# Block inversion through full matrices in DRAM on GpSimd's DMA queue, embeddings' projection by halves, all splits on VectorE

## The chip, the cores and the metric

One core of a Trainium2 chip runs one inference step of a hybrid decoder layer: a prompt of 1024 tokens and 8 sample sequences of 8 tokens. The metric is device time in microseconds, the median over runs; lower is better.

## The reference, cut to what matters

```python
proj = x @ w_in                                   # 1024 -> 3848
o_a, ... = _rwkv7_mix(proj[..., :A_SHIFT_W], ...) # 8 heads of 64: a recurrence over tokens
o_b, ... = _gated_delta_mix(proj[..., A_SHIFT_W:], ...)  # 4 heads of 128, chunks of 64
mix = concat([o_a, o_b]) @ w_o
x = _layer_norm(DN_ALPHA * x + mix, ln1_g, ln1_b)
ffn = (silu(conv(x @ w_gate_half) + b) * (x @ w_up_half)) @ w_down
x = _layer_norm(DN_ALPHA * x + ffn, ln2_g, ln2_b)
e = _rms_norm(p @ w_ple, ple_g)                   # the embeddings' projection
x = x + sigmoid(x @ w_ple_gate) * e
# inside _chunk_gated_delta, per chunk and head:
sol = triangular_solve(eye + Lmat, rhs, lower=True, unit_diagonal=True)
```

The kernel computes the recurrence of mixer A chunk by chunk as well, so both mixers need inverses of unit triangular matrices: per unit of work 24 systems of 64x64.

## The kernel before

**Precision.** A float32 product is made of three passes of float32r: an operand is split into hi and lo (`split`, L257: ACT copies hi, then a subtraction gives lo on VectorE or, without an engine named, on GpSimd). Weights come through `wchunk` (L385), split on VectorE.

**Stages.** The prompt is cut into two token blocks tb of 512. `proj` (L448) projects a block in one gate group and 14 groups of 256 columns (`proj_pair`, 48 matmuls of 128x512 per group) and stores the results to DRAM. The mixers work in units (tb, half, g): 256 tokens, half the heads; eight of them for the prompt, then two for the samples. A unit goes through `prep` (L1042: loads, convolutions, gates, `a_gram` with its Gram products L690, `b_gram`, `invert`), `merge` (L991), `scan` (L1064) and `mix_out` (L1082), which stores into od[tb]. In program order (`run`, L1647 to L1665) the scan of unit i runs with the merge of unit i+1, then comes the output of unit i, then the preparation of unit i+2. The tile framework lays out each engine's order of instructions when the kernel is built, by priorities; buffers of one tag go round in program order. PSUM has 4 banks with the tag acc, 2 aux and 2 scan. Preparation, merge and output all use the aux banks.

**Filler.** Work inside `with s.fill()` has the lowest priority and is to occupy TensorE between the mixers' steps: the projections, the embeddings' projection `ple` (L1364), after unit 3 the output projection `dense_first` of block 0 (L1657; its chunk k needs rows k of od[0], which units 2g and 4+2g store for both halves), then the last projection groups (L1658), `norm_first` and `ffn_first`, in which `ffn_tile` (L1439) copies two columns on GpSimd (L1442, L1444) for each of 22 tiles.

**Inversion.** `invert` (L942) takes a unit's 24 systems. It stores them to a DRAM tile dT (L955), loads their 16x16 diagonal blocks, 4 per system, as 96 rows into iN (L958), inverts all 96 blocks at once on VectorE (L959 to L966), makes a transposed copy (L972), stores both (L967, L973) and loads them back as diagonal blocks of Dd and Dt, 8 DMAs each (L987). The rest of Dd and Dt was set to zero once (L317). All these DMAs go out on the queue `s.uq = nc.scalar` (L311): ScalarE's. `merge` combines the blocks into the full inverse in four rounds of products; `touch` (L204) opens a round with a matmul that waits for the named DMAs. For a sample unit (`small`) the systems are 8x8 blocks, and the inverted blocks go straight into DX (L982, L985).

The embeddings' projection makes, for each token block and column half, one pass of `dense` (L1250) over 2 chunks, with 4 token tiles in 4 acc banks; the banks are emptied by ACT (L1388) at the pass's end.

Of the kernel before, what the change touches and what calls it, by code (L numbers as in the profile page):

```python
# [9 lines left out]
F32 = mybir.dt.float32  # L10
F32R = mybir.dt.float32r
AF = mybir.ActivationFunctionType
ALU = mybir.AluOpType
# [3 lines left out]
D = 1024  # L17
# [128 lines left out]
class Kern:  # L146
# [107 lines left out]
        else:  # L254
            s.act(out, out, AF.Exp, scale=-0.5, bias=s.cst[:p, post:post + 1])

    def split(s, hi, lo, raw, eng=None):  # L257

        s.act(hi, raw)
        s.tt(lo, raw, hi.bitcast(F32), ALU.subtract, eng or s.nc.gpsimd)  # L260

    @contextmanager
    def fill(s):
# [8 lines left out]
    def setup(s):  # L272
        nc, I = s.nc, s.I
        s.cst = s.tl([128, NCST], "cst", pool=s.cp)
        s.par = s.tl([128, NPAR], "par", pool=s.cp)
        s.w2 = s.tl([128, 512], "w2", pool=s.cp)
        s.g2 = s.tl([128, 512], "g2", pool=s.cp)
        nc.scalar.preload_act_table_set("exp_and_others")
        p0 = s.tc.cur_priority
        s.tc.cur_priority = p0 + 200  # L280
        nc.sync.dma_start(s.par, I["par"])
        nc.sync.dma_start(s.cst, I["cst"])
        nc.sync.dma_start(s.w2, I["w2"])
        nc.sync.dma_start(s.g2, I["g2"])
        s.ident = s.cst[:, C_ID:C_ID + 128]
        s.bones = s.cst[:, C_BO:C_BO + 128]
        s.ones = s.cst[:, C_ON:C_ON + 128]
        s.fold = s.cst[:, C_FO:C_FO + 64]
        s.omu = s.tl([128, 14], "omu", pool=s.cp)
        s.ts(s.omu, s.par[:, P_MU:P_MU + 14], -1.0, 1.0, ALU.mult, ALU.add)  # L290
        s.nkk = s.tl([128, 4], "nkk", pool=s.cp)
        s.ts(s.nkk, s.par[:, P_KK:P_KK + 4], -1.0)
        s.oka = s.tl([128, 4], "oka", pool=s.cp)
        s.ts(s.oka, s.par[:, P_KA:P_KA + 4], -0.5, 1.0, ALU.mult, ALU.add)
        s.hpar = s.tl([128, P_KA + 4 - P_W0 + 1], "hpar", pool=s.cp)
        s.ts(s.hpar[:, :P_KA + 4 - P_W0], s.par[:, P_W0:P_KA + 4], 0.5)
        s.ts(s.hpar[:, P_KA + 4 - P_W0:], s.par[:, P_NG:P_NG + 1], 0.5)
        s.eal = s.tl([4, 1], "eal", pool=s.cp)
        s.act(s.eal, s.par[0:4, P_AL:P_AL + 1], AF.Exp)
        s.ts(s.eal, s.eal, -1.0)  # L300
        s.tc.cur_priority = p0
        s.zeros = s.tl([128, 128], "zeros", dt=F32R, pool=s.cp)
        s.act(s.zeros, s.cst[:, C_BM:C_BM + 1].broadcast_to([128, 128]), AF.Copy, scale=0.0)
        s.tails = [s.tl([128, 26, 3], "tail%d" % i, pool=s.cp) for i in range(3)]
        nc.gpsimd.memset(s.tails[-1], 0.0)
        s.od = [s.tl([128, KT, n], "od%d" % i, pool=s.dp) for i, n in enumerate((TB, TB, 64))]
        s.uad = s.tl([128, 14, 8, 8], "uad", pool=s.dp)
        s.ubd = s.tl([128, 12, 8, 8], "ubd", pool=s.dp)
        s.zd = s.tl([128, 4, 64], "zd", pool=s.dp)
        s.SA, s.SB = [], []  # L310
        s.uq = nc.scalar  # L311
        s.iN = s.tl([96, 16, 16], "iN")
        s.iY = s.tl([96, 16, 16], "iY")
        s.it = s.tl([96, 56], "it")
        s.Dd, s.Dt = s.tl([128, 12, 64], "Dd"), s.tl([128, 12, 64], "Dt")
        s.DX = [s.tl([128, 12, LB], "DX%d" % i) for i in range(2)]
        for t in (s.Dd, s.Dt, *s.DX):  # L317
            nc.gpsimd.memset(t, 0.0)
        for g in range(2):
            for S in (s.SA, s.SB):  # L320
                S.append(s.tl([128, 2, 128], "S%d%d" % (g, S is s.SB)))
                nc.gpsimd.memset(S[g], 0.0)
# [33 lines left out]
    def load_x(s, src, more=None):  # L356

        x = s.xtiles()
        if not more and not s.late:
            for k in range(0, KT, 2):  # L360
                raw = s.tl([128, D], "X", 3, dt=F32R, pool=s.c0).bitcast(F32).rearrange("p (k t) -> p k t", k=2)
                s.nc.sync.dma_start(raw, src[:, k:k + 2, :])
                s.split(x[k // 2][:, 0], x[k // 2][:, 1], raw, s.nc.vector if k < 4 else None)
            return x
        for k in range(KT):
            raw = s.hraw() if s.late else s.st()
            with s.tc.high_priority() if more and k < 1 else ExitStack():
                s.nc.sync.dma_start(raw, src[:, k, :])
                s.split(*s.xk(x, k), raw, s.nc.vector if more else None)
                if more and k % 2 == 0:  # L370
                    more(k)
        return x

    def load_xs(s):
        x = s.tl([128, D], "X", 3, dt=F32R, pool=s.c0).rearrange("p (k i t) -> p k i t", k=KT, i=2)
        raw = s.tmp(128, KT, 64)

        def load(k):
            ks = slice(k, k + 2)
            s.nc.sync.dma_start(raw[:, ks], s.I["xT"][:, ks, T:T + 64])  # L380
            s.split(x[:, ks, 0, :], x[:, ks, 1, :], raw[:, ks], s.nc.vector)

        return x, load

    def wchunk(s, src, to=None):  # L385

        w = src.shape[-1]
        raw = s.wraw()
        hi, lo = to or (s.tl([128, 512], t, 3, dt=F32R, pool=s.mp) for t in ("whi", "wlo"))
        with s.tc.high_priority():  # L390
            s.nc.sync.dma_start(raw[:, :w], src)
            s.split(hi[:, :w], lo[:, :w], raw[:, :w], s.nc.vector)
        return hi, lo

    def proj_group(s, x, xs, wsrc, cuts, sample):
# [538 lines left out]
    def systems(s, sa, sb):  # L934

        for h in range(2):
            r = 64 * h
            yield h, 0, sa["MG"].rearrange("p c a s e t -> p (c a) s e t")[r:r + 64, :, 0, 1 - h, :]
            if r < sb["L"]:
                yield h, 2 * sa["nch"], sb["MB"][r:r + 64, :, :, 0, r:r + 64].rearrange("p q h t -> p (q h) t")  # L940

    def invert(s, sa, sb, small):  # L942

        nc = s.nc
        nch = sa["nch"]
        nb = 2 * sb["nq"]
        nh = 2 * nch + nb
        ns = nh + (2 * nch if small else nh)
        dT = s.tl([64, 24, 64], "inv_t", 2, pool=s.dp)
        d1, d2 = (s.tl([96, 16, 16], t, 2, pool=s.dp) for t in ("inv_x", "inv_y"))  # L950
        N, Y, tmp = s.iN, s.iY, s.it
        DX = s.DX[0]
        s.DX = s.DX[::-1]
        for h, y, t in s.systems(sa, sb):
            s.uq.dma_start(dT[:, h * nh + y:h * nh + y + t.shape[1], :], t)  # L955
        n = 4 * ns
        for k in range(4):
            s.uq.dma_start(N[k * ns:(k + 1) * ns], dT[16 * k:16 * k + 16, :ns, 16 * k:16 * k + 16].rearrange("r y t -> y r t"))  # L958
        nc.vector.tensor_copy(Y[:n], N[:n])  # L959
        for j in range(1, 15):  # L960
            m = 15 - j
# [2 lines left out]
            s.mul(t, N[:n, j:j + 1, j + 1:].broadcast_to([n, j, m]), y[:, :, j:j + 1].broadcast_to([n, j, m]))  # L964
            s.add(y[:, :, j + 1:], y[:, :, j + 1:], t)
        nc.vector.memset(Y[:n].rearrange("p a b -> p (a b)")[:, 0::17], 1.0)  # L966
        s.uq.dma_start(d1[:n], Y[:n])  # L967
        if small:
            nc.gpsimd.memset(DX, 0.0)
            todo = ((DX, d1, 64),)  # L970
        else:
            nc.vector.tensor_copy(N[:n], Y[:n].rearrange("p c i -> p i c"))  # L972
            s.uq.dma_start(d2[:n], N[:n])  # L973
            todo = ((s.Dt, d2, 0), (s.Dd, d1, 0))
        for D, d, w in todo:
            for h in range(2):
                for k in range(4):
                    rows = slice(64 * h + 16 * k, 64 * h + 16 * k + 16)
                    cols = slice(w * h + 16 * k, w * h + 16 * k + 16)
                    y = k * ns + h * nh  # L980
                    if small:
                        s.uq.dma_start(D[rows, :2 * nch, cols], d[y:y + 2 * nch].rearrange("y r t -> r y t"))  # L982
                        if h == 0:
                            y += 2 * nch
                            s.uq.dma_start(D[rows, 8:8 + nb, cols], d[y:y + nb].rearrange("y r t -> r y t"))  # L985
                    else:
                        i = s.uq.dma_start(D[rows, :, cols], d[y:y + nh].rearrange("y r t -> r y t"))  # L987
                        sa.setdefault("dma", []).append(i.ins)
        sa["DX"] = sb["DX"] = DX

    def merge(s, sa, sb):  # L991
# [8 lines left out]
        for k in range(4):  # L1000
            bs = [s.bank() for _ in range(2)]
            with s.inrow():
                s.touch(bs[0], s.nc.cur_bb.bb.instructions[-1], *(sa["dma"][8 * k:8 * k + 8] if k < 2 else ()))
                for i in range(12):
                    for h, r in enumerate(halves):
                        s.mm(bs[i // 8][r, i % 8 * 64:i % 8 * 64 + 64], DX[r, i, r] if k else T[h, i],
                             (Dt, Dd, Y, Y)[k][r, i, :])
# [313 lines left out]
    def transposed(s, xs, i, c0, x, tag, dst=None):  # L1321
# [5 lines left out]
        for k in range(0, KT, q):  # L1327
# [16 lines left out]
                hi, lo = (x[k // 2][:, e, :, cs] for e in range(2))  # L1344
                u = u.rearrange("p (k t) -> p k t", k=q)
            s.act(hi, u)
            s.tt(lo, u, hi.bitcast(F32), ALU.subtract, s.nc.gpsimd if (k // q) % 2 else None)

    def transposed_s(s, xs, i, tag):
        x = s.tl([128, KT, 2, 64], "xsm", dt=F32R)  # L1350
# [13 lines left out]
    def ple(s):  # L1364
        nc, I = s.nc, s.I
        for tb in range(3):
# [12 lines left out]
            for h in range(2):  # L1379
# [6 lines left out]
                def evac(t, b):  # L1386
# [1 line left out]
                    s.act(v, b)  # L1388
                    out(4 * tb + t, 128, v)

                s.dense(2, (lambda i: x[i]) if x else None, lambda i: I["w_ple"][h][:, i, :], evac,
                        None if x else (lambda i: xs[:, i]), lambda v: out(8, 64, v))

        mv = s.tl([128, 9, 3], "emv", pool=s.mp)
        nc.vector.memset(mv[:, 8, :], 1.0)
# [332 lines left out]
```

## Time and profile before

| | us |
|---|---|
| median of 3 runs | 1929.57 (1926.03 to 1930.25) |
| the profiled execution | 1927.8 |
| its span | 1926.0 |
| TensorE busy | 1841.5 |
| VectorE busy | 1267.5 |
| ScalarE busy | 920.2 |
| GpSimd busy | 166.8 |

A profile shows one execution. The page gives each engine's busy time, the windows cut it by stretches, the timeline lists instructions in order with what ended the idle time before them, and the waits name who held up whom. PE is TensorE, DVE VectorE, ACT ScalarE, POOL GpSimd and SP SyncE; a q behind the name (ACTq, SPq) marks the issue of a DMA. A granted clock of 1.00 is 2.4 GHz and 0.50 is 1.2 GHz.

### The profile page before, as it was taken

To read this page: it belongs to the slowest core of one execution; us is meant where nothing else is said; L and a number is where in the kernel's file an instruction comes from. 1 tells how busy PE (TensorE), PEld (TensorE's weight loads), DVE (VectorE), ACT (ScalarE), POOL (GpSimd) and SP (SyncE) were. 2 spreads that over 40 slices of the span, in tenths; PEclk is the share of its full clock that TensorE was granted. 3 is DMA by queue.
4 is the path that set the end of the run, shared out by engine and by line. 5 is a ranking of instruction groups with operands and counts; after the bars stand their busy time and mean duration, and the time that the engine had idled before them with its cause. 6 is when DMAs were issued, how large, how long until landed. Compare 5 with 4: busy or idle time off the path is not lost. (4 is left out here: it accounts for less than half of the span.)

```text
span 1926.0 us, 29998 instructions
## 1 busy us (share of the span) xinstructions
PE 1841.5 (96%) x10520; PEld 1475.2 (77%) x10520; DVE 1267.5 (66%) x2711; ACT 920.2 (48%) x1817; POOL 166.8 (9%) x305
## 2 busy tenths in 40 slices
PE   9999999999788899999999999999999999999998
PEld 7878777777667677677877766777788888888877
DVE  4366656848586586877868767666857642555488
ACT  5354538555474644646445534543633332333372
POOL 1000010001000000000000000200212220122000
PEclk9999999999899899999999999999999999999999
DMA  6435432534445265342423445876332222222354
GB/s 215 147 125 154 125 105 79 136 102 132 138 139 152 89 201 179 108 129 83 113 83 107 134 126 190 283 248 206 131 120 94 93 77 83 82 77 81 110 175 165
DMA packets 219127, 255.89 MB, mean 133 GB/s; under 512 B 81848, under 2 KB 117096, under 8 KB 218976
## 3 DMA queue, kind: packets, MB, share of 16 engines
q1 hardware_dynamic: 162040, 246.36, 39.7%
q10 hardware_dynamic: 56936, 7.62, 2.5%
q8 instruction: 83, 1.36, 0.3%
q14 instruction: 68, 0.56, 0.1%
HBM read 200.64 MB, written 53.26 MB: 132 GB/s over the span
## 5 line engine op out<-in xcount | busy, mean ns | idle before, releaser
L190 PE MATMUL acc<-x,whi 128*128 128x512 f32 x2400 | 781.8, 402 | 9.4 <-ACT whi L217 5.1
L220 DVE TENSOR_TENSOR wlo<-wraw,whi 128x512 fp32r<-128x512 f32 (+1 forms) x462 | 331.4, 718 | 350.5 <-ACT whi L217 321.6
L217 ACT ACTIVATE whi<-wraw 128x512 fp32r<-128x512 f32 (+1 forms) x462 | 287.9, 624 | 533.9 <-PE scan L190 203.0
L190 PEld LDWEIGHTS acc<-x,whi 128*128 128x128 f32 x2400 | 429.5, 189 | 92.0 <-issue 8.8
L190 PE MATMUL acc<-x,wlo 128*128 128x512 f32 x1200 | 483.9, 404 | 0.0
L190 PEld LDWEIGHTS acc<-x,wlo 128*128 128x128 f32 x1200 | 226.7, 189 | 53.9 <-issue 5.5
L190 PE MATMUL acc<-whi,X 128*128 128x512 f32 x436 | 145.6, 410 | 9.5 <-ACT st L217 7.5
L190 PEld LDWEIGHTS acc<-whi,X 128*128 128x128 f32 x436 | 82.2, 193 | 30.2 <-issue 5.1
L217 ACT ACTIVATE st<-acc 128x512 f32<-128x512 f32 (+2 forms) x134 | 77.4, 595 | 52.0 <-PE acc L190 30.9
L190 PE MATMUL acc<-wlo,X 128*128 128x512 f32 x220 | 88.1, 402 | 0.0
L229 DVE SCALAR_TENSOR_TENSOR st<-st,par,st 128x512 f32<-128x512 f32 (+1 forms) x132 | 77.9, 592 | 2.1
L190 PE MATMUL scan<-whi,X 128*128 128x256 f32 (+2 forms) x208 | 62.3, 334 | 0.0
L217 ACT ACTIVATE tmp<-tmp 128x512 f32<-128x512 f32 (+4 forms) x75 | 40.5, 548 | 38.4 <-DVE tmp L229 31.5
L217 ACT ACTIVATE st<-st 128x512 f32<-128x512 f32 x66 | 33.4, 505 | 40.4 <-DVE st L229 32.1
L190 PE MATMUL scan<-wlo,X 128*128 128x256 f32 (+2 forms) x164 | 51.3, 313 | 0.0
L217 ACT ACTIVATE tmp<-tmp,par 128x256 f32<-128x256 f32 (+1 forms) x100 | 43.0, 470 | 14.6 <-DMA tmp<-raw_v 3.7
L190 PE MATMUL scan<-whi,xsm 128*128 128x256 f32 x176 | 49.0, 280 | 0.7 <-ACT st L217 0.7
L190 PEld LDWEIGHTS acc<-wlo,X 128*128 128x128 f32 x220 | 42.6, 194 | 9.0
L190 PE MATMUL scan<-wlo,xsm 128*128 128x256 f32 x176 | 49.3, 281 | 0.0
L217 ACT ACTIVATE X<-wraw 128x512 fp32r<-128x512 f32 (+1 forms) x65 | 40.5, 624 | 18.1 <-DMA wraw<-hd 14.3
L220 DVE TENSOR_TENSOR X<-wraw,X 128x512 fp32r<-128x512 f32 x60 | 41.2, 687 | 11.7 <-ACT X L217 11.5
L501 POOL COPY tail<-st 128x3 f32<-128x3 f32 x52 | 13.4, 261 | 401.8 <-ACT st L217 401.8
(355 smaller groups left out, 3334.3 us busy)
## 6 DMA issues: line engine op xcount, KB each, us to landing
wraw<-w_up SPq DMA_DIRECT2D x176, 256.0 KB
wraw<-w_in SPq DMA_DIRECT2D x112, 256.0 KB
wraw<-w_down SPq DMA_DIRECT2D x98, 256.0 KB
wraw<-hd SPq DMA_DIRECT2D x44, 256.0 KB
wraw<-w_o SPq DMA_DIRECT2D x32, 256.0 KB
wraw<-w_gate SPq DMA_DIRECT2D x32, 256.0 KB
hd<-st SPq DMA_DIRECT2D x22, 256.0 KB
st<-lnv SPq DMA_DIRECT2D x20, 256.0 KB
```

Source lines behind the costliest of these rows:

```text
L190: i = s.nc.tensor.matmul(out, lhsT=lhsT, rhs=rhs, start=start, stop=stop)
L217: s.nc.scalar.activation(out, in_, f, **kw)
L220: (eng or s.nc.vector).tensor_tensor(out, a, b, op)
L229: s.nc.vector.scalar_tensor_tensor(out, a, sc, b, op0, op1)
L501: s.nc.gpsimd.tensor_copy(s.tails[tb][:, f0 + f, :], st[:, TB - 3:TB])
```

## The change

All of the inversion's DMAs go out on GpSimd's queue. The stored systems and the inverted blocks are kept in DRAM as full 64x64 matrices of pitch 65*64, so that the four diagonal blocks of a matrix are rows of one regular access pattern (`blocks`) and the whole matrix is another (`sysrows`). The inverted blocks are written into two DRAM tiles dd and dt, whose other elements are set to zero once at the start, and Dd and Dt are read as full matrices: 2 DMAs of 64 partitions each in place of 8 of 16. The transfers over 96 rows are cut into two of 48. The order of the systems changes for prompt units from (half, system) to (system, half). Sample units keep their way into DX, on the new queue.

The embeddings' projection passes over its two chunks for token tiles 0 and 1 first and then for 2 and 3, with the two weight chunks loaded ahead and kept. Every split subtracts on VectorE.

```diff
-    def split(s, hi, lo, raw, eng=None):
+    def split(s, hi, lo, raw):
         s.act(hi, raw)
-        s.tt(lo, raw, hi.bitcast(F32), ALU.subtract, eng or s.nc.gpsimd)
+        s.tt(lo, raw, hi.bitcast(F32), ALU.subtract)
...
-        s.uq = nc.scalar
+        s.uq = nc.gpsimd
...
-        for t in (s.Dd, s.Dt, *s.DX):
+        for t in s.DX:
             nc.gpsimd.memset(t, 0.0)
+        s.dd, s.dt = (s.tl([24, 65 * 64], t, pool=s.dp) for t in ("inv_dd", "inv_dt"))
+        for t in (s.dd, s.dt):
+            for h in range(2):
+                s.uq.dma_start(s.sysrows(t, slice(h, 24, 2)), s.DX[0][64 * h:64 * h + 64, :, 0:64])
...
+    def blocks(s, d, ns):
+        b = d.rearrange("y (k q) -> (y k) q", k=4)[:4 * ns, :16 * 64]
+        return b.rearrange("p (r l) -> p r l", l=64)[:, :, :16]
+
+    def sysrows(s, d, y):
+        return d[y, :64 * 64].rearrange("y (r t) -> r y t", t=64)
...
-        dT = s.tl([64, 24, 64], "inv_t", 2, pool=s.dp)
+        dT = s.tl([24, 65 * 64], "inv_t", 2, pool=s.dp)
...
         for h, y, t in s.systems(sa, sb):
-            s.uq.dma_start(dT[:, h * nh + y:h * nh + y + t.shape[1], :], t)
+            s.uq.dma_start(s.sysrows(dT, of(h, y, t.shape[1])), t)
         n = 4 * ns
-        for k in range(4):
-            s.uq.dma_start(N[k * ns:(k + 1) * ns], dT[16 * k:16 * k + 16, :ns, 16 * k:16 * k + 16].rearrange("r y t -> y r t"))
+        parts = (slice(0, n // 2), slice(n // 2, n))
+        for p in parts:
+            s.uq.dma_start(N[p], s.blocks(dT, ns)[p])
...
-            nc.vector.tensor_copy(N[:n], Y[:n].rearrange("p c i -> p i c"))
-            s.uq.dma_start(d2[:n], N[:n])
-            todo = ((s.Dt, d2, 0), (s.Dd, d1, 0))
...
-                        i = s.uq.dma_start(D[rows, :, cols], d[y:y + nh].rearrange("y r t -> r y t"))
-                        sa.setdefault("dma", []).append(i.ins)
+            nc.vector.tensor_copy(N[:n], Y[:n].rearrange("p c i -> p i c"))
+            for X, d, D in ((N, s.dt, s.Dt), (Y, s.dd, s.Dd)):
+                for p in parts:
+                    s.uq.dma_start(s.blocks(d, ns)[p], X[p])
+                for h in range(2):
+                    i = s.uq.dma_start(D[64 * h:64 * h + 64], s.sysrows(d, slice(h, 24, 2)))
+                    sa.setdefault("dma", []).append(i.ins)
...
-                s.touch(bs[0], s.nc.cur_bb.bb.instructions[-1], *(sa["dma"][8 * k:8 * k + 8] if k < 2 else ()))
+                s.touch(bs[0], s.nc.cur_bb.bb.instructions[-1], *sa["dma"][2 * k:2 * k + 2])
...
-                s.dense(2, (lambda i: x[i]) if x else None, lambda i: I["w_ple"][h][:, i, :], evac,
-                        None if x else (lambda i: xs[:, i]), lambda v: out(8, 64, v))
+                W = [s.wchunk(I["w_ple"][h][:, i, :]) for i in range(2)]
+                s.dense(2, (lambda i: x[i]) if x else None, None, evac, None if x else (lambda i: xs[:, i]),
+                        lambda v: out(8, 64, v), parts=((0, 1), (2, 3)) if x else ((),), kept=W)
```

## Rows read from the trace of the kernel before

**Rows 1.** The page, parts 1 and 5: busy time by engine; the commonest matmul.
```profile
PE 1841.5 (96%) x10520; PEld 1475.2 (77%) x10520; DVE 1267.5 (66%) x2711; ACT 920.2 (48%) x1817; POOL 166.8 (9%) x305
...
L190 PE MATMUL acc<-x,whi 128*128 128x512 f32 x2400 | 781.8, 402 | 9.4 <-ACT whi L217 5.1
```

**Rows 2.** Windows: stretch, width; PE, PEld, DVE, ACT, POOL busy; PEclk, DMA, GB/s.
```profile
611.00:660.00 49.00, 34.14 (x299) 25.69 (x298) 16.46 (x32) 20.60 (x36) 0.19 (x1) 0.79 0.28 78
```

**Rows 3.** Waits of PE over the span: us in total, times, longest.
```profile
PE acc L190 <- ACT st L217: 11.2, 6, 4.7
PE aux L190 <- DMA Dt<-inv_y: 9.4, 2, 7.7
PE aux L190 <- DMA Dd<-inv_x: 7.8, 3, 5.6
```

**Rows 4.** Timeline of ACT's DMA issues, unit 4's inversion: start, us, what.
```profile
580.75 0.62 ACTq L955 DMA_DIRECT2D inv_t<-MG  x1
...
585.68 1.25 ACTq L955 DMA_DIRECT2D inv_t<-MB  x2
589.96 1.27 ACTq L958 DMA_DIRECT2D iN<-inv_t  x3
592.61 0.30 ACTq L958 DMA_DIRECT2D iN<-inv_t  x1
610.19 0.33 ACTq L967 DMA_DIRECT2D inv_x<-iY  x1
...
613.98 0.32 ACTq L987 DMA_DIRECT2D Dd<-inv_x  x1
614.39 5.00 ACTq L987 DMA_DIRECT2D Dt<-inv_y  x8
```

**Rows 5.** Timeline of DVE, unit 4's inversion: its first and last copy.
```profile
596.64 0.28 DVE L959 COPY iY<-iN 96x256 f32<-96x256 f32 x1
...
610.19 0.38 DVE L972 COPY iN<-iY 96x256 f32<-96x256 f32 x1
```

**Rows 6.** Timeline of PE, 611 to 660 us; in brackets the idle time before.
```profile
621.12 0.35 PE L190 MATMUL aux<-zeros 128*128 128x8 f32 x1 [5.62 <-DMA Dd<-inv_x]
...
624.91 0.34 PE L190 MATMUL aux<-zeros 128*128 128x8 f32 x1 [0.69 <-DVE DX L220]
...
639.07 1.08 PE L190 MATMUL aux<-OA,cst 128*128 128x512 f32 x2
...
657.13 0.79 PE L190 MATMUL acc<-whi,X 128*128 128x512 f32 x1
```

**Rows 7.** Timeline of PE: unit 3's merge, gate_rows of block 1, unit 4's Gram products.
```profile
501.09 1.97 PE L190 MATMUL aux<-Dt,MG 64*64 64x64 f32 x32
...
526.16 1.16 PE L214 MATMUL aux<-cst,tmp 4*128 4x4 f32 x16
...
573.13 1.16 PE L190 MATMUL aux<-AR,BK 64*128 64x128 f32 x16
```

**Rows 8.** Timeline of SP's DMA issues, 610 to 720 us.
```profile
650.71 0.33 SPq L1468 DMA_DIRECT2D wraw<-od  x1
...
715.13 4.96 SPq L391 DMA_DIRECT2D wraw<-w_in  x4
```

**Rows 9.** Groups by line and form: the split of 128x512, POOL and DVE.
```profile
L220 POOL TENSOR_TENSOR hl<-st,hh 128x512 fp32r<-128x512 f32 x22 | 28.5, 1295 | 55.5 <-ACT hh L217 55.5
...
L220 DVE TENSOR_TENSOR X<-wraw,X 128x512 fp32r<-128x512 f32 x60 | 41.2, 687 | 11.7 <-ACT X L217 11.5
```

**Rows 10.** Timelines of POOL and DVE at 251 us.
```profile
251.42 2.40 POOL L220 TENSOR_TENSOR x<-X,x 128x1024 fp32r<-128x1024 f32 x1 [7.99 <-ACT x L217]
...
251.56 2.42 DVE L959 COPY iY<-iN 96x256 f32<-96x256 f32 x1 [2.48 <-DMA iN<-inv_t]
```

**Rows 11.** Timeline of SP: the last sample unit's store, the first load after it.
```profile
1191.17 0.42 SPq L929 DMA_DIRECT2D od<-otmp  x1
...
1224.72 0.42 SPq L368 DMA_DIRECT2D hraw<-od  x1
```

More of the change, by code (lines that the diff above doesn't have):

```diff
@@ L362, in load_x @@
                 s.nc.sync.dma_start(raw, src[:, k:k + 2, :])
-                s.split(x[k // 2][:, 0], x[k // 2][:, 1], raw, s.nc.vector if k < 4 else None)
+                s.split(x[k // 2][:, 0], x[k // 2][:, 1], raw)
             return x
@@ L368, in load_x @@
                 s.nc.sync.dma_start(raw, src[:, k, :])
-                s.split(*s.xk(x, k), raw, s.nc.vector if more else None)
+                s.split(*s.xk(x, k), raw)
                 if more and k % 2 == 0:
@@ L380, in load @@
             s.nc.sync.dma_start(raw[:, ks], s.I["xT"][:, ks, T:T + 64])
-            s.split(x[:, ks, 0, :], x[:, ks, 1, :], raw[:, ks], s.nc.vector)
+            s.split(x[:, ks, 0, :], x[:, ks, 1, :], raw[:, ks])
         return x, load
@@ L391, in wchunk @@
             s.nc.sync.dma_start(raw[:, :w], src)
-            s.split(hi[:, :w], lo[:, :w], raw[:, :w], s.nc.vector)
+            s.split(hi[:, :w], lo[:, :w], raw[:, :w])
         return hi, lo
@@ L948, in invert @@
         ns = nh + (2 * nch if small else nh)
-        dT = s.tl([64, 24, 64], "inv_t", 2, pool=s.dp)
-        d1, d2 = (s.tl([96, 16, 16], t, 2, pool=s.dp) for t in ("inv_x", "inv_y"))
+        dT = s.tl([24, 65 * 64], "inv_t", 2, pool=s.dp)
         N, Y, tmp = s.iN, s.iY, s.it
@@ L953, in invert, with of @@
         s.DX = s.DX[::-1]
+        def of(h, y, n):
+            return slice(h * nh + y, h * nh + y + n) if small else slice(2 * y + h, 2 * (y + n) + h - 1, 2)
         for h, y, t in s.systems(sa, sb):
-            s.uq.dma_start(dT[:, h * nh + y:h * nh + y + t.shape[1], :], t)
+            s.uq.dma_start(s.sysrows(dT, of(h, y, t.shape[1])), t)
         n = 4 * ns
-        for k in range(4):
-            s.uq.dma_start(N[k * ns:(k + 1) * ns], dT[16 * k:16 * k + 16, :ns, 16 * k:16 * k + 16].rearrange("r y t -> y r t"))
+        parts = (slice(0, n // 2), slice(n // 2, n))
+        for p in parts:
+            s.uq.dma_start(N[p], s.blocks(dT, ns)[p])
         nc.vector.tensor_copy(Y[:n], N[:n])
@@ L966, in invert @@
         nc.vector.memset(Y[:n].rearrange("p a b -> p (a b)")[:, 0::17], 1.0)
-        s.uq.dma_start(d1[:n], Y[:n])
         if small:
+            d = s.tl([96, 16, 16], "inv_x", 2, pool=s.dp)
+            s.uq.dma_start(d[:n], Y[:n])
+            d = d.rearrange("(y k) r t -> k r y t", k=4)
             nc.gpsimd.memset(DX, 0.0)
-            todo = ((DX, d1, 64),)
-        else:
-            nc.vector.tensor_copy(N[:n], Y[:n].rearrange("p c i -> p i c"))
-            s.uq.dma_start(d2[:n], N[:n])
-            todo = ((s.Dt, d2, 0), (s.Dd, d1, 0))
-        for D, d, w in todo:
             for h in range(2):
@@ L978, in invert @@
                     rows = slice(64 * h + 16 * k, 64 * h + 16 * k + 16)
[L979 to L986, printed above, removed]
-                        i = s.uq.dma_start(D[rows, :, cols], d[y:y + nh].rearrange("y r t -> r y t"))
-                        sa.setdefault("dma", []).append(i.ins)
+                    y = h * nh
+                    s.uq.dma_start(DX[rows, :2 * nch, rows], d[k, :, y:y + 2 * nch, :])
+                    if h == 0:
+                        s.uq.dma_start(DX[rows, 8:8 + nb, rows], d[k, :, 2 * nch:nh, :])
+        else:
+            nc.vector.tensor_copy(N[:n], Y[:n].rearrange("p c i -> p i c"))
[5 more added lines that the diff above has]
+                    sa.setdefault("dma", []).append(i.ins)
         sa["DX"] = sb["DX"] = DX
@@ L1346, in transposed @@
             s.act(hi, u)
-            s.tt(lo, u, hi.bitcast(F32), ALU.subtract, s.nc.gpsimd if (k // q) % 2 else None)
+            s.tt(lo, u, hi.bitcast(F32), ALU.subtract)
     def transposed_s(s, xs, i, tag):
```

## The prediction

> **What bounds the kernel now.** I read the page's busy times first: TensorE (PE) is busy 1841.5 of 1926.0 us [rows 1], so at most 84.5 us of the span are PE's idle time, and an edit that moves work between VectorE (DVE), ScalarE (ACT) and GpSimd (POOL) matters only where PE waits for it. The windows then say where that is. One stretch stands out: from 611 to 660 us PE is busy 34.14 of 49 us at a mean granted clock of 0.79 [rows 2], that is, part of it at 1.2 instead of 2.4 GHz, after PE had sat idle. Idle and clock together make this hole worth about 14.9 + 0.21 x 49 = 25 us. The list of waits names the first releaser: PE waited 9.4 us for Dt and 7.8 us for Dd, the inversion's last loads, and 11.2 us for ACT's copies out of the acc banks [rows 3].
>
> The timelines tell why the hole cannot be filled. A unit's inversion is a serial path: ACT issues the stores of the systems, the loads of the diagonal blocks, the stores of the inverted blocks and 16 loads into Dt and Dd [rows 4], with about 14 us of DVE work between the copies L959 and L972 [rows 5]. PE's first merge product of unit 4 waits until 621.12, and unit 3's output follows only at 639.07 [rows 6], because it takes its aux banks behind merge's (program order, L1074 to L1079 and L1652). The next unit's preparation follows that output in turn: merge of unit 3 at 501.09, gate_rows' transposes of tb=1 at 526.16, the Gram products of unit 4 at 573.13 [rows 7]. So all five inversions of units 0 to 4 lie one behind the other on the path to od[0]. dense_first (L1657) has four acc banks and needs od[0] chunk 2, which unit 3's output stores; its load goes out at 650.71 [rows 8] and PE resumes at 657.13 [rows 6]. The last two projection groups (the w_in loads at 715.13 [rows 8]) are 2 x 48 matmuls of 402 ns [rows 1], 38.6 us, but they are queued behind dense_first.
>
> Hence the rule of this case: time saved on filler before 611 us only lengthens the hole; time added to one inversion is paid about five times.
>
> **The change part by part.** *The inversion.* It replaces 4+4+2+16 = 26 transfers on ACT's queue by 4+2+4+4 = 14 on POOL's. What the rows show of unit 4 [rows 4 to 6]: the two MB stores take 585.68 to 586.93, their landing 3.03 us (to the first iN load at 589.96), the four iN issues 2.95 us, their landing 3.73 us (to L959 at 596.64). Behind DVE's work: the store of Y at 610.19 lands 3.46 us after its issue ends (first Dd load 613.98), eight Dt issues end at 619.39, and PE starts 1.73 us later. Dd costs nothing: at 624.91 merge waits for DVE, not for it.
>
> After, with c for one POOL transfer of 768 runs (64 B or 256 B pieces) and m for one of 256: the head ends at 585.68 + 2m + 3.03 + 2c + 3.73; for the tail I take the four stores as issued together ahead of the reads, since both are ready within 0.4 us: 610.19 + 4c + 3.46 + 2c + 1.73 = 615.38 + 6c, against 621.12 now. The tail breaks even at c = 0.96 us. No row shows a transfer issued by POOL, so c is bounded.
> - From below: ACT's own issue of 512 runs, 0.62 us [rows 4]; the head ends 1.7 us and the tail 2.0 us earlier, 3.7 us per inversion.
> - From above: each transfer is issued only when the one before it has landed, 0.62 + 3.03 = 3.65 us; head +10.4 and tail +16.2, and Dd, two reads later than Dt, is then late too (7.3 against the 3.8 us that merge's first round covers): about +30 us per inversion.
> - Taken: ACT's 0.62 times POOL's slowness on the same 128x512 split, 1295 against 687 ns [rows 9], gives 1.17 us if runs don't count and 1.75 if the price grows with 768/512; c = 1.46, the middle, and m = 1.17. The head ends at 597.7 (+1.1), the tail at 624.1 (+3.0): +4.1 us per inversion, 20 us for the five.
>
> The Trainium skill bears on this on two sides. "SBUF — State Buffer", section "SBUF: two separate sides", says that a DMA issued from GpSimd needs descriptors that GpSimd writes itself, and that a VectorE copy in a two-port mode locks it out; no run here shows that, but [rows 10] show the two engines holding each other. By that rule the copies of 0.28 and 0.38 us and their like would add about 1 us per inversion, 5 us in all, and the sum would be some 1955.
>
> What replaces the gain on ACT: its queue is rid of 26 issues per inversion, but between 614 and 621 us, where it did nothing else, PE had no filler left. I cost that relief at nothing. The zeroing of the DRAM matrices (4 transfers) runs before POOL's first tail copy and long before the first inversion; nothing. Behind waiting transfers on POOL's queue stand the memsets of UV (L678) and DX (L997), the tail copies (L501) and ffn_tile's copies (L1442, L1444). The last hold a DVE chain that frees an acc bank; PE's cover is the next group, 48 x 402 ns = 19.3 us [rows 1], against some 10 to 15 us in which POOL may stand on a landing: nothing, and a few us per unit if the cover is gone.
>
> Units 5 to 7 and the two sample units (12 reads each at c, about +8 us) come after od[0]: 3 x 4.1 + 16 = 28 us more. Their last store is issued at 1191.17 and its reader only at 1224.72 [rows 11], 33 us later: hidden.
>
> *Splits.* Before 660 us DVE takes over two of 128x1024 and four of 128x512 from POOL, about 8 x 0.687 = 5.5 us [rows 9], perhaps half of it on the path: +2.8. It loses the collision at 251.5, where the copy L959, 0.28 us elsewhere, took 2.42 beside POOL's split [rows 5, 10]: -2.1. Net +0.7. Later moves (44 in the second FFN, the transposes) lie where PE is busy throughout; within 2 us either way.
>
> *Embeddings by halves.* Same matmuls; two of four banks are emptied half a pass earlier. It can take some of the 11.2 us [rows 3], all filler time ahead of the hole: nothing.
>
> **Sum.** 1927.8 us (this execution; 1.8 us beside its span) + 20.3 + 0.7 = 1948.8. The median of the runs is 1.8 us above this execution: 1950.6, rounded 1950.
>
> **Rivals.**
> 1. *POOL's queue is cheap* (ends faster). From c below 0.96 us the tail shortens. At 0.62: 5 x 3.7 = 18.5 us off, within the hole's 25: 1929.6 - 18.5 + 0.7 = 1912. For it: fewer transfers, and the 16 reads' 5 us of Dt issue are a real part of the path. Against it: POOL is the slower engine in every row that it shares with DVE. The Trainium skill, "DMA: Bandwidth & Descriptors", section "Anatomy of one DMA — SWDGE (gpsimd) path", is on this side: of about 2 us fixed it gives most to completion and little to generation; no run here shows it. Chance 0.22.
> 2. *The rebuilt order fills the hole* (faster). If PE's order, laid down anew around slower transfers, puts the two left-over groups (38.6 us) ahead of dense_first, then even a hole 20 us longer is filled; 25 us off, about 1905. Against it: dense_first is first in the program and its first chunk is ready early. Chance 0.12.
> 3. *POOL's transfers follow one another only after landing*, c from 2.2 up. At 2.5 (m = 2): head +4.8, tail +9.3 and Dd +1.2, 15 us per inversion, 1929.6 + 76 = 2005; at 3.65 about 2080, less the 38.6 us of left-over groups if they come first. For it: consecutive transfers of one shape on one queue. Against: on ACT's queue the issues follow one another without landing [rows 4]. Chance 0.11.
> 4. *It breaks even* (c near 1, or gains in the filler stretch that shorten the path after all): within 0.2%. Chance 0.09.
> The forecast, c between 1.1 and 2.2 (1.1 us to 12 us per inversion), 1936 to 1990, has 0.46.
>
> **How the numbers follow.** Slower: 0.46 + 0.11 = 0.57; within 0.2%, about what a measurement of this kernel can tell from no change, 0.09; faster 0.22 + 0.12 = 0.34. The range leaves out most of rival 3 and the best of rivals 1 and 2, about 0.1 on each side: 1903 to 1992. As both signs have much of the chance: the forecast's own range is 1936 to 1990.
>
> **What would show it.** In the changed profile: the first Dt product of unit 4 later than 621 us and the interval from L972 to it above 11 us (right), below 10 us (rival 1); PE's busy share between unit 3's last projection group and dense_first's resumption below 70% (right), near full (rival 2); gaps of 3 us between one POOL transfer and the next (rival 3). I am wrong in the mechanism if the inversions take longer and the time does not follow fivefold, or if it follows without them.

## The result and the profile after

The changed kernel takes 2045.23 us (2045.09 to 2045.84, 4 runs) against 1929.89 before, a ratio of 1.0602 (95% interval 1.0583 to 1.0621): 115 us slower. The forecast had the sign right and the size wrong: 1950, range 1903 to 1992.

Part 1 and part 3 of the page of after: busy time by engine; the DMA queue that the inversion now uses. It answers [rows 1].

```profile
PE 1863.6 (91%) x10520; PEld 1494.4 (73%) x10520; DVE 1272.9 (62%) x2787; ACT 915.1 (45%) x1812; POOL 172.6 (8%) x379
...
q0 software_dynamic: 6272, 12.94, 2.7%
```

The span is 2043.1 us, so TensorE idles 179.5 us where it idled 84.5 [rows 1]: 95.0 us of the 117.1 that the span grew. The other 22.1 us are in its busy time, for the same 10520 instructions: more of the matmuls ran at the lower clock, after idle stretches (mean granted clock 0.958 against 0.985). Neither POOL's busy time nor its queue's share tells of a trouble; both are small.

The waits of PE in after (us in total, times, longest), against [rows 3]:

```profile
PE aux L190 <- DMA Dt<-inv_dt: 94.3, 8, 15.3
...
PE scan L190 <- DVE S L220: 19.4, 6, 6.2
...
PE acc L190 <- ACT st L217: 5.5, 3, 3.0
...
PE aux L190 <- DMA Dd<-inv_dd: 1.0, 2, 0.7
```

Dt and Dd cost 95.3 us where they cost 17.2: 78 of the 95 us of new idle time stand in these two lines, nearly all of it in the eight waits for Dt, one for each prompt unit. The timeline of POOL in unit 4's inversion, against [rows 4], says why Dt is late (start, us, what; in brackets the idle time before it):

```profile
640.40 0.74 POOL L977 DMA_DIRECT2D iN<-inv_t  x1 [4.42 <-ACT QE L217]
...
643.26 1.26 POOL L973 DMA_DIRECT2D inv_t<-MB  x2 [1.56 <-DVE wlo L220]
...
662.13 0.73 POOL L1002 DMA_DIRECT2D inv_dd<-iY  x1 [13.93 <-DVE iY L220]
667.95 0.74 POOL L1002 DMA_DIRECT2D inv_dt<-iN  x1 [5.08 <-issue]
671.00 0.74 POOL L1002 DMA_DIRECT2D inv_dt<-iN  x1 [2.31 <-issue]
673.75 0.74 POOL L1002 DMA_DIRECT2D inv_dd<-iY  x1 [2.01 <-issue]
674.49 0.32 POOL L505 COPY tail<-st 128x3 f32<-128x3 f32 x2
676.50 0.77 POOL L1004 DMA_DIRECT2D Dt<-inv_dt  x1 [1.69 <-issue]
680.08 0.76 POOL L1004 DMA_DIRECT2D Dt<-inv_dt  x1 [2.82 <-issue]
```

Each transfer keeps POOL busy for about 0.75 us, and before the next it stands idle for 2 to 5 us with nothing that the profile shows as its cause ("issue"), though the four stores have had their data since the end of DVE's second copy:

```profile
650.24 0.29 DVE L978 COPY iY<-iN 96x256 f32<-96x256 f32 x1 [4.85 <-DMA iN<-inv_t]
...
661.76 0.38 DVE L999 COPY iN<-iY 96x256 f32<-96x256 f32 x1
```

From 662.13 to 680.08 there are five steps of 3.59 us on average. In this stretch the transfers of one kind land a median of 2.6 to 4.0 us after their issue, so the spacing is about the time in which one lands. The two MB stores, of 256 runs each, follow one another with no gap.

PE in the same stretch, against [rows 6], and its windows (columns as in [rows 2]); the touch is the matmul aux<-zeros:

```profile
668.31 0.39 PE L190 MATMUL acc<-x,wlo 128*128 128x512 f32 x1
683.63 0.34 PE L190 MATMUL aux<-zeros 128*128 128x8 f32 x1 [14.93 <-DMA Dt<-inv_dt]
683.91 1.97 PE L190 MATMUL aux<-Dt,MG 64*64 64x64 f32 x32
685.67 1.06 PE L190 MATMUL aux<-Dt,MB 64*64 64x64 f32 x16
686.66 1.22 PE L190 MATMUL acc<-x,whi 128*128 128x512 f32 x2
```

```profile
660.00:684.00 24.00, 9.07 (x41) 7.11 (x41) 5.76 (x14) 3.02 (x6) 4.99 (x9) 0.76 0.38 102
684.00:722.00 38.00, 32.94 (x300) 24.23 (x301) 16.07 (x30) 19.49 (x34) 1.73 (x4) 0.81 0.31 96
```

The touch waits 14.93 us, and filler matmuls (acc<-x,whi) stand right behind the first merge products, at 686.66. Filler had not run out: it comes later in PE's order, and PE cannot pass the touch. The mean granted clock is 0.76 in the stretch with the idle time and still 0.81 in the 38 us after it, so a part of each ran at 1.2 GHz, after PE had sat idle.

### The profile page after: what moved, and what is told of

The parts are those of the page before. It is cut to its first block, busy times and chain, and to the rows that moved or that the text cites. A ratio compares the mean times of both kernels' runs of the same rounds, so it can differ in the third digit from the quotient of the medians.

```text
span 2043.1 us, 29880 instructions
## 1 busy us (share of the span) xinstructions
PE 1863.6 (91%) x10520; PEld 1494.4 (73%) x10520; DVE 1272.9 (62%) x2787; ACT 915.1 (45%) x1812; POOL 172.6 (8%) x379
## 4 chain that ended last, share of the span: by engine, by line
PE 43%; DMA 4%; DVE 4%; issue 3%; ACT 1%; POOL 0%; SPq 0%; DVEq 0%; ACTq 0%; POOLq 0%
PE acc L190 27%; PE scan L190 9%; PE aux L190 6%; DMA wraw<-w_o 1%; DVE wlo L220 1%; DMA wraw<-hd 1%; DVE st L229 0%; DMA tmp<-uad 0%; PE aux L214 0%; DMA st<-lnv 0%; DVE X L220 0%; DMA Dt<-inv_dt 0%; DMA wraw<-w_gate 0%; DMA iN<-inv_t 0%; DMA x2t<-u 0%
## 5 line engine op out<-in xcount | busy, mean ns | idle before, releaser
L190 PE MATMUL acc<-x,whi 128*128 128x512 f32 x2400 | 790.9, 405 | 8.0 <-ACT whi L217 5.2
L220 DVE TENSOR_TENSOR wlo<-wraw,whi 128x512 fp32r<-128x512 f32 (+1 forms) x462 | 314.4, 682 | 346.3 <-ACT whi L217 315.0
L190 PE MATMUL aux<-zeros 128*128 128x8 f32 x60 | 17.4, 289 | 98.3 <-DMA Dt<-inv_dt 94.3
L190 PEld LDWEIGHTS aux<-zeros 128*128 128x128 f32 x60 | 12.3, 205 | 112.1 <-issue 99.9
L220 DVE TENSOR_TENSOR DX<-aux,cst 64x512 f32<-64x512 f32 (+1 forms) x32 | 17.8, 555 | 91.6 <-PE aux L190 91.1
L220 DVE TENSOR_TENSOR X<-wraw,X 128x512 fp32r<-128x512 f32 (+1 forms) x65 | 44.3, 681 | 14.5 <-ACT X L217 14.4
L217 ACT ACTIVATE tmp<-tmp,par 128x256 f32<-128x256 f32 (+1 forms) x100 | 43.1, 470 | 15.8 <-DVE tmp L517 7.3
```

Source lines behind the costliest of these rows:

```text
L190: i = s.nc.tensor.matmul(out, lhsT=lhsT, rhs=rhs, start=start, stop=stop)
L217: s.nc.scalar.activation(out, in_, f, **kw)
L220: (eng or s.nc.vector).tensor_tensor(out, a, b, op)
```

## The experiments

Theory A: GpSimd's queue has room for a certain number of runs in flight, one transfer of 768 fills it, and the next waits until that one has drained. The rivals: the layout of full matrices is slow on any queue (B); VectorE's copies keep GpSimd from issuing (C); the embeddings or the splits cost the time (D); every GpSimd transfer waits for the one before it, whatever its size (A'). The ratios are to runs of the kernel before on the chip of the run itself (1931.7 us for x1 to x4 and 1932.0 for x5 to x8, 1932.6 for x9 to x12).

| run | us | ratio to before (95%) |
|---|---|---|
| x1: all of the change, queue ScalarE | 1934.7 | 1.0019 (1.0006 to 1.0032) |
| x2: all of the change, twice the room | 1947.4 | 1.0088 (1.0063 to 1.0114) |
| x3: before, queue GpSimd | 1999.0 | 1.0345 (1.0329 to 1.0360) |
| x4: before, halves and splits | 1921.6 | 0.9939 (0.9919 to 0.9958) |
| x5: as x1, zeroing on GpSimd | 1926.5 | 0.9980 (0.9964 to 0.9995) |
| x6: before, halves | 1935.5 | 1.0020 (1.0004 to 1.0035) |
| x7: before, splits | 1915.7 | 0.9918 (0.9897 to 0.9939) |
| x8: as x5, GpSimd for units 0 to 4 | 2001.5 | 1.0369 (1.0350 to 1.0388) |
| x9: as x5, GpSimd for units 5 to 7 and samples | 1980.6 | 1.0252 (1.0234 to 1.0271) |
| x10: x5 without the halves | 1935.7 | 1.0017 (1.0002 to 1.0032) |
| x11: before, the second FFN's splits | 1930.1 | 0.9989 (0.9972 to 1.0006) |
| x12: control of x2 | 2053.0 | 1.0627 (1.0603 to 1.0652) |

**x1, the queue or the layout.**

```diff
-        s.uq = nc.gpsimd
+        s.uq = nc.scalar
```

> The changed kernel with its inversion's transfers issued by ScalarE instead of GpSimd (one word); full matrices, embeddings by halves and splits on VectorE stay. Theory A (what cost the time is GpSimd's queue, where a 768-run transfer starts only some 3.1 to 3.7 us after the one before it): about 14 issues of 0.6 to 1.9 us on ScalarE, the waits of TensorE for Dt fall from 94 us to under 25, time 1915 to 1950. Rival B (the full matrices with their short runs are slow on any queue): the touches still wait over 8 us each, 2010 to 2050. Rival D (the embeddings and the splits cost the time): 2030 to 2050.

1934.7 us, and the waits for Dt are 15.0 us. B and D fall: with one word the 115 us go down to 3. The issues of unit 4's tail on ScalarE:

```profile
620.74 0.31 ACTq L1002 DMA_DIRECT2D inv_dd<-iY  x1
621.16 1.05 ACTq L1002 DMA_DIRECT2D inv_dt<-iN  x2
622.26 0.55 ACTq L1002 DMA_DIRECT2D inv_dd<-iY  x1
624.18 1.32 ACTq L1004 DMA_DIRECT2D Dt<-inv_dt  x2
```

The same transfers follow one another at 0.3 to 0.7 us, but for a pause of 1.4 us between the stores and the loads. From the copy L999 (620.74) to the touch (628.52) pass 7.8 us, against 21.9 in after and 10.9 before [rows 5, 6]. The framework lays out another order of PE's work for this kernel; x2 keeps that of after.

**x2, the room alone.** The order of PE's matmuls is that of after, so here nothing differs but the queue's room and the width of the touch, for which x12 is the control.

```diff
-    nc = _bacc.Bacc("TRN2", ..., dynamic_dma_scratch_size=1024)
+    nc = _bacc.Bacc("TRN2", ..., dynamic_dma_scratch_size=2048)
...
-        i = s.mm(b[:, 0:8], s.zeros, s.zeros[:, 0:8])
+        i = s.mm(b[0:8, 0:8], s.zeros, s.zeros)      # zeros is 128x8
```

> The changed kernel with dynamic_dma_scratch_size 2048 in place of 1024 (the room is taken from the constant of zeros that the touch matmuls read, 8 columns in place of 128; the order of TensorE is the same). Theory A (GpSimd's queue has room for the runs of one 768-run transfer, so the next waits until that one has drained): two transfers are now in flight, pairs follow one another within about 1 us, the touch of unit 4 comes 14 to 16 us after the copy L999 in place of 21.9, PE's waits for Dt fall from 94 to 20 to 50 us, time 1960 to 2010. Rival C (VectorE's copies keep GpSimd from issuing) and rival B (landing of this layout is slow by itself): gaps of 3 us stay, time 2035 to 2050.

1947.4 us: 98 of the 115 us go, 13 us more than the expectation's better end. The cleanest place is the start of the program, where four zeroing transfers of 768 runs wait for nothing but the queue. First after, then x2:

```profile
3.56 0.93 POOL L322 DMA_DIRECT2D inv_dd<-DX  x1
8.64 0.77 POOL L322 DMA_DIRECT2D inv_dd<-DX  x1 [4.15 <-issue]
14.08 0.76 POOL L322 DMA_DIRECT2D inv_dt<-DX  x1 [4.67 <-issue]
18.76 0.76 POOL L322 DMA_DIRECT2D inv_dt<-DX  x1 [3.93 <-issue]
```

```profile
3.56 1.68 POOL L322 DMA_DIRECT2D inv_dd<-DX  x2
9.38 0.77 POOL L322 DMA_DIRECT2D inv_dt<-DX  x1 [4.14 <-issue]
10.91 0.76 POOL L322 DMA_DIRECT2D inv_dt<-DX  x1 [0.77 <-issue]
```

With twice the room two go back to back, and the third waits. Unit 4's tail in x2 shows the same pairs, the touch comes 14.3 us after the copy L999 (604.34 to 618.64) instead of 21.9, and waits 4.12 us instead of 14.93:

```profile
604.71 0.73 POOL L1002 DMA_DIRECT2D inv_dd<-iY  x1 [8.77 <-DVE iY L220]
605.44 0.74 POOL L1002 DMA_DIRECT2D inv_dt<-iN  x1
609.07 0.73 POOL L1002 DMA_DIRECT2D inv_dt<-iN  x1 [2.89 <-issue]
611.09 0.74 POOL L1002 DMA_DIRECT2D inv_dd<-iY  x1 [1.29 <-issue]
...
613.78 1.51 POOL L1004 DMA_DIRECT2D Dt<-inv_dt  x2 [1.63 <-DMA inv_dt<-iN]
```

C falls as the cause of these gaps: VectorE makes the same copies here. By the Trainium skill, "SBUF — State Buffer", section "SBUF: two separate sides", a VectorE copy in a two-port mode keeps GpSimd from writing descriptors; gaps made by that would have stayed. What that lock may still cost beside them is not told apart.

**x12, the control.** x2's narrow touch with the room as it was.

> The control for x2: the changed kernel with the touch matmuls on 8 columns of zeros, as in x2, but with the queue's room as it was (1024). If x2's gain of 98 us is the room's and not the touch's, this is the changed kernel again: 2040 to 2050, waits for Dt 90 to 98 us. If the touch carried it: near 1950.

2053.0 us, 3 us above the expected range, and the wait is that of after, so the touch carried nothing of x2's gain:

```profile
PE aux L190 <- DMA Dt<-inv_dt: 93.3, 8, 14.7
```

**x3, small transfers on the same queue.**

```diff
-        s.uq = nc.scalar
+        s.uq = nc.gpsimd
```

> The kernel before with nothing changed but the queue of the inversion's transfers, GpSimd in place of ScalarE: 26 transfers of 96 to 512 runs. Theory A (the gap on GpSimd's queue comes from the runs in flight: several transfers of 192 runs fit side by side): the 16 loads into Dt and Dd follow one another at 0.7 to 1.2 us, the inversion is 0 to 8 us longer than on ScalarE, time 1930 to 1990. Rival A' (every GpSimd transfer waits for the landing of the one before it, whatever its size): 26 x 3.4 us, some 50 us more for each inversion, time over 2150. The prediction's c (1.17 to 1.75 us each) would give about 16 x 0.6 = 10 us more for each inversion, 1970 to 2010.

1999.0 us, between A and A', at the place that the prediction's c would have given, though for another reason. POOL in unit 4, loads of 384 runs (iN) and of 192 (Dt):

```profile
612.63 0.75 POOL L958 DMA_DIRECT2D iN<-inv_t  x1 [0.42 <-issue]
615.20 0.70 POOL L958 DMA_DIRECT2D iN<-inv_t  x1 [1.82 <-issue]
618.42 0.69 POOL L958 DMA_DIRECT2D iN<-inv_t  x1 [2.52 <-issue]
620.92 0.68 POOL L958 DMA_DIRECT2D iN<-inv_t  x1 [1.81 <-issue]
...
639.43 1.64 POOL L987 DMA_DIRECT2D Dt<-inv_y  x3 [0.21 <-issue]
642.35 2.21 POOL L987 DMA_DIRECT2D Dt<-inv_y  x4 [1.28 <-issue]
```

Loads of 192 runs go out three and four in a row, 0.55 us each, and then pause. A' falls. The tail, from L972 (635.92) to the touch (648.91), is 13.0 us, 2 more than before. But loads of 384 runs stand 2.5 to 3.2 us apart, so the head pays: from the first MB store (608.05) to the copy L959 (623.37) 15.3 us against 11.0 [rows 4, 5]. A had overlooked these four loads, and its range was 9 us too low. That two of 384 don't go as a pair where one of 768 finds room says that the room is no plain count of runs; how it is counted stays open.

**x4, x6, x7, x11, the other two parts.**

```diff
# x6: ple
-  s.dense(2, ..., lambda i: I["w_ple"][h][:, i, :], evac, ...)
+  W = [s.wchunk(I["w_ple"][h][:, i, :]) for i in range(2)]
+  s.dense(2, ..., None, evac, ..., parts=((0, 1), (2, 3)) if x else ((),), kept=W)
# x7: split, and the transposes' subtraction
-  s.tt(lo, raw, hi.bitcast(F32), ALU.subtract, eng or s.nc.gpsimd)
+  s.tt(lo, raw, hi.bitcast(F32), ALU.subtract)
...
-  s.tt(lo, u, hi.bitcast(F32), ALU.subtract, s.nc.gpsimd if (k // q) % 2 else None)
+  s.tt(lo, u, hi.bitcast(F32), ALU.subtract)
# x11: the splits of H and HS alone get s.nc.vector; x4 is x6 and x7 together
```

> The kernel before with the other two parts of the change alone: embeddings' projection by halves and all splits on VectorE; the inversion stays as it was. Theory A: they carry nothing of the 115 us, 1922 to 1940 (the prediction costed them at +0.7 us). Rival D (they hold VectorE in the units and so the whole path): 1960 to 2045.

> The kernel before with the embeddings' projection by halves alone. x4 (halves and splits) was 0.6% faster than before, 11.7 us. The prediction put the halves at nothing: 1926 to 1934. Rival (the halves carry x4's gain by freeing acc banks earlier): 1915 to 1924.

> The kernel before with all splits on VectorE alone. The prediction put this at +0.7 us: 1926 to 1934. Rival (the splits carry x4's gain: 128x512 takes 0.69 us on VectorE against 1.30 on GpSimd, and the collisions of the two engines go): 1915 to 1924. If neither x6 nor x7 is below 1925, x4's gain comes of the two together, through the order that is laid down anew.

> The kernel before with only the 44 splits of the second FFN's hidden tiles (128x512 and 128x64) moved from GpSimd to VectorE. The prediction: they lie where TensorE is busy throughout, within 2 us of before, 1929 to 1935. x7 gained 16 us with all splits; by its windows some 6 us of that lie before 400 us and 3 us between 1250 and 1600. Rival (the second FFN carries it): 1915 to 1924.

x4 gives 1921.6, so D falls once more. Of its parts the halves cost 3.6 us and the splits gain 16.3, so x7, at 1915.7, is the fastest kernel here; both lie outside the 1926 to 1934 of the prediction. Together the two gain 10.1 (x4), somewhat less than their sum. x11 shows that the 44 splits of the second FFN are not what gains: 2.5 us, not told from nothing, as predicted. The windows of before, then of x7, up to 400 us:

```profile
0.00:400.00 400.00, 386.12 (x2401) 315.49 (x2402) 235.22 (x535) 205.33 (x416) 25.31 (x66) 0.99 0.45 137
```

```profile
0.00:400.00 400.00, 391.95 (x2558) 320.44 (x2559) 235.92 (x544) 205.98 (x416) 21.02 (x64) 1.00 0.46 138
```

PE does 5.8 us more there. Splits on GpSimd collided with VectorE on the inversions' path, and there were more of them than [rows 10] show. In before, POOL's second split, with a DVE step of the inversion that takes 0.20 us in x7:

```profile
255.22 2.65 POOL L220 TENSOR_TENSOR x<-X,x 128x1024 fp32r<-128x1024 f32 x1 [1.40 <-ACT x L217]
```

```profile
255.60 2.34 DVE L220 TENSOR_TENSOR it<-iN,iY 96x44 f32<-96x44 f32 x1
```

```profile
254.89 0.20 DVE L220 TENSOR_TENSOR it<-iN,iY 96x44 f32<-96x44 f32 x1
```

Three more of POOL's splits, at 441.89, 446.55 and 484.28, lie beside unit 3's preparation and inversion. The copy L972 comes 3.1 us earlier in x7 in unit 1 (263.45 against 266.59), 9.0 in unit 2, 10.9 in unit 3 (479.36 against 490.29), 7.9 in unit 4 (602.25 against 610.19) and 5.6 to 6.3 in units 5 to 7. Unit 2, first before, then x7:

```profile
385.92 0.38 DVE L972 COPY iN<-iY 96x256 f32<-96x256 f32 x1
```

```profile
376.91 0.39 DVE L972 COPY iN<-iY 96x256 f32<-96x256 f32 x1
```

So most of unit 3's lead stands already in unit 2, and between the copies of units 1 and 2 POOL had no split in before. From 270 us on the order of PE's work differs between the two kernels. The collisions account for some 5 us of the lead (3.1 in unit 1, 1.9 more in unit 3); where the rest of the 16.3 us comes from stays open.

**x8 and x9, which units pay.**

```diff
# in invert, first lines (x9 with the two queues exchanged)
+        s.uq = nc.gpsimd if s.ninv < 5 else nc.scalar
+        s.ninv += 1
```

> All of the change, but the inversion's transfers go by GpSimd for units 0 to 4 only; units 5 to 7 and the samples use ScalarE. The prediction's rule (only the five inversions ahead of od[0] lie on the path, the later ones are hidden): nearly all of the 115 us stay, 2015 to 2045. Rival (every unit pays, because TensorE waits in program order at each merge, 60 of 94 us of the waits for Dt before unit 5 and 34 from it on): 1985 to 2012.

> The converse of x8: the inversion's transfers of units 5 to 7 and of the two sample units go by GpSimd, those of units 0 to 4 by ScalarE. The prediction hid all of this behind 33 us of slack up to the reader of od[0]: 1924 to 1935, like x5 at 1926.5. Rival (TensorE waits in program order at the merges of units 5 to 7 too; after has 34.4 us of waits there, and x8 paid 72 us for 60.3 us of waits): 1926.5 + 25 to 50, that is 1950 to 1975.

x8 lies in its rival's range and x9 6 us above its own; both are far from the prediction's rule. Against x5 (1926.5) the first five inversions on GpSimd cost 75 us and the last three with the samples 54; together 129, and after is 119 above x5. So each inversion costs some 15 to 18 us wherever it stands, with the samples' share, which was not tried apart, counted to the last three. The order of PE's work goes with the queue: up to unit 5's preparation x8 has that of after and x9 that of x5, and the price includes it. x9's touches of units 5, 6 and 7:

```profile
753.45 0.35 PE L190 MATMUL aux<-zeros 128*128 128x8 f32 x1 [13.29 <-DMA Dt<-inv_dt]
...
886.37 0.35 PE L190 MATMUL aux<-zeros 128*128 128x8 f32 x1 [10.03 <-DMA Dt<-inv_dt]
...
1002.38 0.34 PE L190 MATMUL aux<-zeros 128*128 128x8 f32 x1 [10.76 <-DMA Dt<-inv_dt]
```

**x5 and x10, the layout on ScalarE.**

```diff
# x5, against x1 (x10: the same without the halves)
-                s.uq.dma_start(s.sysrows(t, slice(h, 24, 2)), s.DX[0][...])
+                nc.gpsimd.dma_start(s.sysrows(t, slice(h, 24, 2)), s.DX[0][...])
```

> As x1 (all of the change, transfers of the inversion on ScalarE), but the four zeroing transfers stay on GpSimd's queue. x1 lost some 7 us of TensorE's work before 145 us against x4, at a granted clock of 0.96 instead of 1.00, and its chain from the copy L999 to the first Dt product of unit 4 took 7.8 us against 9.6 in x4. Theory: the zeroing on ScalarE's queue ahead of the first casts costs the start, and the layout by itself saves about 2 us for each inversion: 1910 to 1922. Rival: the start is not the zeroing's, or the layout gains nothing: 1925 to 1938.

> The splits on VectorE and the full-matrix layout with its transfers on ScalarE (zeroing on GpSimd), without the embeddings' halves. x7 (splits alone) had 1915.7. If the parts add (x5 against x4: the layout on ScalarE +4.9 us; x4 against x7: the halves +6.0): 1918 to 1924. Rival (x4 to x5 was the order laid down anew around the halves, and the layout saves 2 us per inversion where the halves are gone): 1904 to 1914.

The zeroing off ScalarE's queue is worth 8 us (x1 to x5). PE's work before 145 us, 134.0 us in x1 against 140.2 in x5, points the same way, but the profiled execution of x1 took 1941.2 us, 6.6 above its median, so that row alone would not show it. The layout itself gains nothing: x5 is 4.9 us above x4 and in its rival's range, and x10, 20 us above x7, is slower than both of its ranges. Yet x5's tail in unit 4 is 8.0 us (605.35 to 613.30) against 10.9 before. Why a shorter inversion ends in a longer time stays open; PE's order was laid down anew in these kernels, and that was not tried apart. Two things stand in the traces: PE comes to unit 4's touch so much earlier that it waits there for 11.24 us in x5 against 3.02 in x4, and its waits for ACT's copies into tmp add up to 10.7 us against 4.1.

## Why the prediction was wrong

1. **The price c of a POOL transfer** is a term that was mis-sized: 1.46 us against 3.59. What was scaled is the time in which POOL works on a transfer, and for that even the lower bound of 0.62 us [rows 4] was near (0.63 to 0.77). The spacing comes of what follows it: the runs in flight (x2, x12). That was rival 3, given 0.11, whose upper price of 3.65 us was near; "on ACT's queue the issues follow one another without landing" was no evidence for another queue. It is not landing as such that counts either: with twice the room two transfers go at once.
2. **The form of the sum.** Tail 615.38 + 6c at 3.59 would be 15.8 us later; measured from the copy to the touch it is 10.9 longer. Six transfers have only five steps between them, and the landing of the stores lies inside the steps: 0.37 + 5 x 3.59 + 3.55, from the last load's start to the touch, is 21.87 us. The head, put at +1.1, grew by 0.4: from MB's end on VectorE to the copy of the blocks 12.1 us (638.11 to 650.24) against 11.7 (584.94 to 596.64, [rows 5]). First after, then before:

```profile
636.82 1.29 DVE L220 TENSOR_TENSOR MB<-aux,tmp 128x512 f32<-128x512 f32 x2
```

```profile
583.65 1.29 DVE L220 TENSOR_TENSOR MB<-aux,tmp 128x512 f32<-128x512 f32 x2
```

   Counted from the first MB store, as in the prediction, the head looks shorter (7.0 us against 11.0), but on POOL's queue that store stands behind the first iN load, which goes out at 640.40 only. Unit 4's inversion is thus 11.3 us longer where 4.1 were forecast.
3. **Fivefold, and units 5 to 7 hidden** [rows 11]: wrong, and this fails by itself: five times 11.3 us would be 57 us, some 1986, within the stated range. The price is paid in all eight units (x8, x9); eight times 11.3 is 90 us, near the 95.0 of new idle time, and the 22.1 us of busy time at the lower clock, which the sum did not have for the new waits, come on top. The slack of 33 us was counted to the reader of od[0], but PE waits before that, at the touch, in the order laid down at the build. The hole before [rows 2, 6] was one of missing filler; the new waits are not, for filler stands right behind them. With c = 3.59 and m = 0.63 the prediction's sum would have given +4.2 and +15.8, fivefold 100 us: near the measured 115 by luck, with an inversion 8.7 us too long and three units left out.
4. **Rival 2, the rebuilt order**: it did not fill the hole. PE is busy 9.07 of 24 us up to unit 4's touch, and 32.94 of the 38 us after it at a mean clock of 0.81.
5. **VectorE's copies**, +5 us by the rule in "SBUF: two separate sides" of the Trainium skill's page "SBUF — State Buffer": not seen as the cause (x2). **Rival 1** drew on the Trainium skill, "DMA: Bandwidth & Descriptors", section "Anatomy of one DMA — SWDGE (gpsimd) path", for a cheap issue. The traces agree on the issue (0.63 us for 256 runs, 0.75 for 768), but a queue that lets one transfer drain before the next does not show in that account.
6. **Splits**, +0.7 forecast, -16.3 measured (x7): the step counted one collision (-2.1, [rows 10]) and took half of the moved work onto the path. Five such splits lay beside the work of two units, but by the copies' times the collisions make up some 5 us; the larger part first shows in unit 2, where none lay, and is not explained. The later moves within 2 us: the 44 of the second FFN measured -2.5 (x11), no contradiction; the transposes' were not tried alone.
7. **The halves** at nothing: +3.6 us (x6), at the limit of what can be told from no change. **Zeroing** at nothing: right on POOL (PE's work before 145 us is 140.2 us in x5 and 140.4 in x4, which has no zeroing), 8 us on ScalarE.
8. **The signs.** "First Dt product later than 621" (683.91) and "interval above 11 us" (22.2) came true, and "gaps of 3 us" named rival 3. "Busy share below 70%" came true too (9.07 + 32.94 of 62 us, 68%), but the kernel before had 70% already [rows 2]. The sign for a wrong mechanism, a time that does not follow fivefold, came true as well: fivefold would have had x9 at 1926.

## What to carry to other kernels

An engine's busy time for a DMA says little of how often its queue can take one: before a chain of transfers is moved to another queue, look for two consecutive ones on it with all data ready, and read the spacing, for the size of transfer that is meant. Where the order of an engine is fixed at build time, a delay is paid at the place where it waits, even when filler stands behind it and the data's last reader is far off. Parts of a change that were made together are worth trying alone: here one of three carried a gain of 0.8% that the others hid.

## What was not expected of the hardware

- A GpSimd transfer of 768 runs keeps its queue for 3.6 us in unit 4's tail and for 4.7 to 5.4 us at the start of the program; with dynamic_dma_scratch_size 2048 two go at once. At 1024, 384-run loads stand 2.5 to 3.2 us apart and 192-run loads go out up to four in a row at 0.55 us.
- ScalarE takes the same 768-run transfers at 0.3 to 0.7 us each (x1).
- Beside a GpSimd split a small VectorE operation of the inversion took 2.34 us instead of 0.20, as the copy in [rows 10] did.
